# A transformer block on one core: operands of two pairs of features stay on chip between gate/up and down, weight loads move ahead of the next splits, and down's sums are stored two products later

## The chip, the cores and the metric

The kernel runs on one core of one Trainium2 chip. The core has five engines with a queue each: TensorE (PE, with its weight loads shown apart as PEld), VectorE (DVE), ScalarE (ACT), GpSimd (POOL) and SyncE (SP), which here only issues DMA transfers. The engines meet through semaphores. The metric is the device time of one execution in microseconds (us); the time before is the median of three executions.

## The reference

One layer of a decoder block over T = 512 tokens with 2048 channels, in float32:

```
h    = rms_norm(x, norm1_g)
proj = h @ w_in                     # split into heads of three token mixers
mix  = concat(dilated attention A, conformer convolution B, sliding attention C)
x    = x + mix @ w_out
h2   = rms_norm(x, norm2_g)
x    = x + (silu(h2 @ w_gate) * (h2 @ w_up)) @ w_down
```

The feed-forward width is 5632, that is 44 tiles of 128 features. The last line is the part in which the change lies. Its two stages are called gate/up and down here.

## The kernel before

**Precision.** A product of float32 operands is made from a high part (a copy to the type float32r) and a low part (the operand less its high part). For weights `split_up_to` makes them: ACT copies the weight to PSUM (`wn`, line 240) and to SBUF (`wh`, line 241), and DVE subtracts (`wl`, line 242). There are three buffers of each, and the split of a product is made two products ahead (`SPLIT_AHEAD`).

**Seven products in place of eight.** Gate/up and down multiply 2 x 2 blocks with a scheme of seven products, in the order `ORDER = (5, 1, 7, 6, 2, 4, 3)`. The 44 feature tiles are 22 *pairs* (tile p and tile p + 22); the 16 channel tiles are 8 pairs. A block of gate/up (`Wide`) is one pair of features of gate or of up: g0, u0, g1, u1, ... u21, so 44 blocks of seven products. A product is a run of matmuls of 128x512 with `wh` and one of 128x256 with `wl`, eight of each; the order of the two runs flips from product to product. A block of down (`Down`) is one pair of output tiles over a window of six to eight pairs of features. There are 24: three sweeps over the eight output pairs, and the list `DOWN` gives the windows, (0..5), (0..6), (1..7) and so on. The third sweep runs into pair 22, which is pair 0 again. Block d0 has 12 matmuls in a product, d1 has 14.

**Weights.** `group` lists, for each block, four raw weights to load (21, 22, 11, 12) and four sums over them, which are some of the seven factors: s = 21 + 22 four products before the block's first product, 21 += 11 three before, s -= 11 (in effect) at the first, s += 12 two after. They run on POOL, except for the group named `g0`, whose sums run on DVE. The raw weights lie in seven buffers by name; `pump` issues loads on SP for as long as the next entry's buffer is free. `next_unit` is called once per product: it runs the sums that are due, splits the weight of two products on, and then calls `pump`.

**Order within a product.** There is no scheduler: each engine runs its instructions in the order of the program (`manual_schedule`), so that the order of the calls sets the order in every queue. For each product the loop at the end of the kernel calls the sums, then `run(evacs)` (the previous product's results out of PSUM), then `next_unit`, then `multiply`, and then `run(extras)`. `later(n, ...)` puts a call n products further on in one of the two lists.

**Operands of down.** At the end of an up block, POOL, ACT and DVE make the seven operands of the pair from the four blocks of its result: `sums1` and `sums2` (POOL) and `piece1` to `piece4`. A piece makes one or two operands of high and low part (128x512 each) in a *stage* tile, of which there are two, and stores them to DRAM (`od[p]`, line 940 in the profile for the issue). `load_act` (issue at line 1116) brings operands back as tiles of 256 KB, `a{q}_{j}` for product q and pair j, in a pool of 71 *slots* of 2 KB per partition. A slot also holds normalised inputs, results and the y tiles, so the loads for d0 are called product by product in the last block of gate/up, as its inputs `ops` are dropped: six loads a product, 42 in all. Later blocks of down load the pairs that are new to their window. `load_y` reads the running sum of two output tiles (`x2d`) ahead of each block, `Down.done` adds to it, and `Down.store` writes it back, `later(0, ...)` on the list `extras`, that is in the same product.

**One queue.** All these transfers are issued by SP in the order of the program: raw weights (line 211), operands (1116), stage tiles (940), y (1069), and sums (1083).

Of the kernel before, what the change touches and what calls it, by code (L numbers as in the profile page):

```python
# [9 lines left out]
F32 = mybir.dt.float32  # L10
F32R = mybir.dt.float32r
# [4 lines left out]
P = 128  # L16
T = 512
# [26 lines left out]
        "bg3 ak2 cq4 ak0 av0 cq6 aq0 ak1 av1 aq1 av2 aq2 ak3 av3 aq3").split()  # L44
ROWS = "c0 c1 c2 c4 c5 c3 c7 c6 a0 a1 b2 b1 b0 b3 a2 a3".split()

N_SLOTS = 71

RAW_PLAIN = "22b sb 21 22a 11 sa 12".split()
RAW_BUFS = 7  # L50
RAW_EARLY = 5
# [11 lines left out]
TH = T // 2  # L63
NJ = KT // 2
NP = NF // 2


_A = [0, 0, 1, 2, 3, 4, 5, 6]
_B = [_A[n] + (6 if n == 0 else 7) for n in range(8)]
_C = [b + 8 for b in _B]  # L70
DOWN = [(n, *w) for ab in (zip(_A, _B), zip(_B, _C), zip(_C, [a + NP for a in _A])) for n, w in enumerate(ab)]

LAID = (5, 7, 6, 4, 3, 1, 2)
# [36 lines left out]
def kernel(ctx: ExitStack, tc: tile.TileContext, xT, wi, wo, wgu, wd, cst_in, outT):  # L110
    nc = tc.nc
    cp = ctx.enter_context(tc.tile_pool(name="consts", bufs=1))
    wp = ctx.enter_context(tc.tile_pool(name="weights", bufs=1))
    sp = ctx.enter_context(tc.tile_pool(name="slots", bufs=N_SLOTS))
    ctx.enter_context(tc.manual_schedule())
# [14 lines left out]
    def slot(name, dt=F32, cols=T):  # L130
        return sp.tile([P, cols], dt, name=name, tag="s")

    def bank(name, cols=T):
        return psum["banks"].tile([P, cols], F32, name=name, tag="b")
# [11 lines left out]
    def take(buf, key, n=1024):  # L146
        assert buf not in held
        held[buf] = key
        raws[key] = (wp.tile([P, 1024], F32, name=f"w{key}", tag=f"raw{buf}", bufs=1), n)
        return raws[key][0]  # L150

    def drop(key):
        for buf in [b for b, k in held.items() if k == key]:
            held.pop(buf)
        return raws.pop(key)
# [29 lines left out]
        works.extend((key[k], last, None) for k, last in (  # L185
            ("s", False), ("11", False), ("21", True), ("s", False), ("12", True), ("22", True), ("s", True)))

    for p in range(NP):
        for m in range(2):
            group(f"{'gu'[m]}{p}", m, 1024, {f"{i + 1}{k + 1}": [wgu[4 * (p + i * NP) + 2 * m + k]]  # L190
                                             for i in range(2) for k in range(2)})

    def down_block(n, half, first, end):

        parts = [(first, min(end, NP)), (0, end - NP)] if first < NP else [(first - NP, end - NP)]
        return [bass.AP(tensor=wd.tensor, offset=wd.offset + (n * P * NF + half * NP + a) * P,
                        ap=[[NF * P, P], [1, (b - a) * P]]) for a, b in parts if b > a]
# [6 lines left out]
    at = {"entry": 0, "split": 0, "use": 0}  # L204

    def pump(limit):
        while at["entry"] < len(entries) and len(raws) < limit and entries[at["entry"]][0] not in held:
            buf, key, parts = entries[at["entry"]]
            t, o = take(buf, key, sum(p.shape[-1] for p in parts)), 0
            for part in parts:  # L210
                nc.sync.dma_start(t[:, o:o + part.shape[-1]], part)
                o += part.shape[-1]
            at["entry"] += 1


    lows, late_lows = [], []

    def lows_now():
        while lows:
            fn, *args = lows.pop(0)  # L220
            fn(*args)  # L221
        if late_lows:
            pump(RAW_EARLY if at["use"] <= 20 else RAW_BUFS)

    def split_up_to(i):
        while at["split"] <= min(i, len(works) - 1):
            key, last, eng = works[at["split"]]
            t, n = drop(key) if last else raws[key]
            u = at["split"]
            hi = wp.tile([P, 1024], F32R, name=f"wh{u}", tag="hi", bufs=SPLIT_BUFS)  # L230
            lo = wp.tile([P, 1024], F32R, name=f"wl{u}", tag="lo", bufs=SPLIT_BUFS)
            if eng or "high" not in psum:
                eng = eng or nc.vector
                nc.scalar.copy(hi[:, :n], t[:, :n])  # L234
                lows.append((eng.tensor_sub, lo[:, :n], t[:, :n], hi[:, :n].bitcast(F32)))
                if not late_lows:
                    lows_now()
            else:
                near = psum["high"].tile([P, 1024], F32R, name=f"wn{u}", tag="h")
                nc.scalar.copy(near[:, :n], t[:, :n])  # L240
                nc.scalar.copy(hi[:, :n], t[:, :n])  # L241
                nc.vector.tensor_sub(lo[:, :n], t[:, :n], near[:, :n].bitcast(F32))
            splits[u] = (hi, lo)
            at["split"] += 1

    def sums_now():
        for fn in sums.pop(at["use"], ()):
            fn()

    def next_unit():  # L250
        sums_now()
        u = at["use"]
        at["use"] += 1
        lows_now()
        split_up_to(u + SPLIT_AHEAD)
        if not lows:
            pump(RAW_EARLY if u < 20 else RAW_BUFS)
        return splits.pop(u)

    def mm3(out, wh, wl, xh, xl, start, stop):  # L260
# [14 lines left out]
    for k in range(X_AHEAD):  # L275
        load_first(k)
        u = k if k < 2 else k // 2 + 1
# [100 lines left out]
    for k in range(KT):  # L378
# [9 lines left out]
        hi, lo = h_hl.pop(k)  # L388
# [14 lines left out]
    def project(name):  # L403
        b = bank(name)
        for half in range(2):
            wh, wl = next_unit()
            for kk in range(8):
                k = 8 * half + kk
                s = slice(kk * P, (kk + 1) * P)
                mm3(b, wh[:, s], wl[:, s], h_hi[k], h_lo[k], k == 0, k == KT - 1)  # L410
                if kk == 3:
                    lows_now()
                if kk % 2 == 1:
                    ticks.tick()
        return b
# [357 lines left out]
    for name in PROJ[HEAD4:]:  # L773
        kind, what, j = name[0], name[1], name[2:]
# [3 lines left out]
        b = project(name)  # L778
# [19 lines left out]
    b = box = boxes = shared = None  # L798
# [84 lines left out]
    for half in range(2):  # L883
        for i, n in enumerate(OUT_ORDER[half]):
            if half == 1 and i == 2:
                ticks.drain()
                b = None
                open_banks(banks=4, high=2)
            b = bank(f"o{half}_{n}")
            wh, wl = next_unit()  # L890
            for kk in range(8):
                k = 8 * half + kk
# [4 lines left out]
                s = slice(kk * P, (kk + 1) * P)  # L897
# [29 lines left out]
    def norm2b():  # L927
# [2 lines left out]
        nc.scalar.copy(R_12, b)  # L930
        nc.scalar.copy(r2b[:, T:], b[:, :TH])

    od = {p: tc.dram_tile([P, 7 * T], F32, name=f"od{p}") for p in range(NP)}
    evacs, extras = [], []
    flip = [1]
# [6 lines left out]
    def later(n, fn, *args, queue=evacs):  # L942
        while len(queue) <= n:
            queue.append([])
        queue[n].append((fn, *args))
# [35 lines left out]
    class Wide(Block):  # L981
# [54 lines left out]

        def piece(self, at, src):
            n = src.shape[-1] // TH
            both = wp.tile([P, 2 * T], F32R, name=f"{self.name}st{at}", tag="stage", bufs=2)
            near = psum["high"].tile([P, 1024], F32R, name=f"{self.name}n{at}", tag="h")[:, :n * TH]  # L1040
            hi, lo = (both[:, :n * T].rearrange("p (a b c) -> p a b c", a=n, b=2)[:, :, b] for b in range(2))
            src2, near2 = (t.rearrange("p (a b) -> p a b", a=n) for t in (src, near))
            nc.scalar.copy(near, src)
            nc.scalar.copy(hi, src2)
            nc.vector.tensor_sub(lo, src2, near2.bitcast(F32))
            later(0, nc.sync.dma_start, od[self.p][:, at * T:(at + n) * T], both[:, :n * T].bitcast(F32), queue=extras)

        def piece1(self):
            self.piece(0, self.ta)
# [21 lines left out]
    class Down(Block):  # L1071
# [9 lines left out]
        def store(self, n, t, cols):  # L1081
            def go():
                nc.sync.dma_start(self.out[n][:, cols], t[:, cols])
            if self.tail:
                go()
            else:
                later(0, go, queue=extras)

        def done(self, q):
            one, two = slice(0, TH), slice(TH, T)  # L1090
# [16 lines left out]
                self.add(q, t[:, cols])  # L1107
                self.store(n, t, cols)

    acts = {}  # L1110

    def load_act(q, pairs):
        for j in pairs:
            acts[q, j] = slot(f"a{q}_{j}", F32R)
            at = LAID.index(q)
            nc.sync.dma_start(acts[q, j].bitcast(F32), od[j % NP][:, at * T:(at + 1) * T])

    blk = gate = None
    for g in range(2 * NP + len(DOWN)):
        t = g - 2 * NP  # L1120
        if t < 0:
            p, m = divmod(g, 2)
            blk = Wide(p, m, gate if m else None)
            gate = blk if m == 0 else None
        else:
            n, first, end = DOWN[t]
            blk = Down(t)
        for i, q in enumerate(ORDER):
            sums_now()
            run(evacs)  # L1130
            w = next_unit()
            if t < 0:
                blk.multiply(q, w, [ops[q, j] for j in range(NJ)])
            else:
                blk.multiply(q, w, [acts[q, j] for j in range(first, end)])
            if g == 0 and i in (2, 3):
                (norm2a if i == 2 else norm2b)()

            if t == -1:
                for j in range(NJ):  # L1140
                    ops.pop((q, j))
                later(1, load_act, q, range(*DOWN[0][1:]), queue=extras)
            elif 0 <= t < len(DOWN) - 1:
                for j in range(first, DOWN[t + 1][1]):
                    acts.pop((q, j))
                later(1, load_act, q, range(end, DOWN[t + 1][2]), queue=extras)
            if t >= -1 and i == 3:
                load_y(t + 1)
            run(extras)
# [85 lines left out]
```

## Time and profile before

| | us |
|---|---|
| median of three executions | 1929.6 (1929.41 to 1929.71) |
| the profiled execution's own time | 1929.75 |
| its span, from the first instruction to the last | 1928.0 |
| PE busy | 1898.0 (98% of the span) |
| DVE, ACT, POOL busy | 1469.7, 1329.9, 985.9 |
| gate/up on PE | 623.0 to 1481.65 |
| down on PE | 1481.65 to about 1924.2 |
| waits of PE for operands from `od` | 5.3 in 13 waits, the longest 2.4 |
| loads of operands, `a<-od` | 196 of 256.0 KB, 5.4 us from issue to landing |

Reading it: a line of the profile names the program line, the engine, the operation, and output and inputs by the program's names; "x6" is a count of instructions that stand together, and what stands in brackets is the engine's idle time ahead of the instruction and what ended it. "L966" is the one line of all matmuls of gate/up and down; `out<-h` are those of gate/up and `out<-a` those of down. The clock is the share of its full rate that TensorE was granted. Weights are named by kind and block: `w('22', 'd1')` is the raw weight 22 of block d1. A chain in order of time gives start, duration, and what ran or was waited for.

### The profile page before, as it was taken

The page shows a single profiled execution, that of the slowest core. Times are in us where ns is not written, and L with a number is a line of the kernel's source. Part 1 is how long each engine was busy: PE and PEld are TensorE (multiplying, and loading weights), DVE is VectorE, ACT ScalarE, POOL GpSimd, SP SyncE. Part 2 cuts the span into 40 slices and gives each one's busy share as a digit, 9 for nine tenths or more (in the row PEclk, how much of TensorE's full clock was granted, in tenths as well). Part 3 has the DMA queues.
Part 4 walks back from the last instruction along what each step waited for, and adds up shares of the span by engine and source line. Part 5 has one row for each costly group of instructions (what it writes and reads, how often), then busy time and mean ns, then how long its engine had stood idle before and what let it go on. Part 6 is the DMA issues. An engine that isn't in the chain of part 4 may idle for free.

```text
span 1928.0 us, 29223 instructions
## 1 busy us (share of the span) xinstructions
PE 1898.0 (98%) x10332; PEld 1643.8 (85%) x10332; DVE 1469.7 (76%) x2512; ACT 1329.9 (69%) x1782; POOL 985.9 (51%) x636
## 2 busy tenths in 40 slices
PE   8999999999999999999999999999999999999999
PEld 7888788878877888888888888888888788888888
DVE  6799989997468777777777777777777577767776
ACT  6356555553356888788888888888887677667675
POOL 0111011000000788788887878788876666656564
PEclk9999999999999999999999999999999999999999
DMA  7222232223342344444444444454438988777685
GB/s 264 85 97 66 66 88 77 72 77 126 121 128 80 134 156 164 138 161 166 159 143 156 161 157 155 138 180 142 170 126 302 365 276 278 264 248 270 201 277 195
DMA packets 125651, 319.48 MB, mean 166 GB/s; under 512 B 14016, under 2 KB 29504, under 8 KB 125504
## 3 DMA queue, kind: packets, MB, share of 16 engines
q1 hardware_dynamic: 125360, 317.51, 48.1%
q8 instruction: 81, 1.33, 0.3%
q14 instruction: 66, 0.54, 0.1%
q10 hardware_dynamic: 144, 0.10, 0.0%
HBM read 259.09 MB, written 57.15 MB: 164 GB/s over the span
## 4 chain that ended last, share of the span: by engine, by line
PE 66%; DMA 1%; DVE 0%; ACT 0%; issue 0%; DVEq 0%; SPq 0%
PE out L966 66%; DMA a<-od 1%; DMA od<-u21st 0%; ACT wn L240 0%; DVE h L873 0%; ACT wh L241 0%; DVE ssum L90 0%; DVE xr L823 0%; PE n2b L301 0%; ACT h L867 0%; ACT h L833 0%; ACT sr L843 0%; PE r2s L307 0%; DVE tb L860 0%; DVE y L978 0%
## 5 line engine op out<-in xcount | busy, mean ns | idle before, releaser
L966 PE MATMUL out<-h,wh 128*128 128x512 f32 x2464 | 588.5, 391 | 3.6 <-DVE h L873 3.6
L966 PEld LDWEIGHTS out<-h,wh 128*128 128x128 f32 x2464 | 452.9, 188 | 91.6 <-DVE h L873 4.1
L966 PEld LDWEIGHTS out<-h,wl 128*128 128x128 f32 x2464 | 317.4, 192 | 12.0
L966 PE MATMUL out<-h,wl 128*128 128x256 f32 x2464 | 321.4, 284 | 0.0
L966 PE MATMUL out<-a,wh 128*128 128x512 f32 x1232 | 299.6, 393 | 3.5 <-DMA a<-od 3.1
L966 PEld LDWEIGHTS out<-a,wh 128*128 128x128 f32 x1232 | 226.9, 189 | 50.5 <-DMA a<-od 3.8
L234 ACT CAST wh<-w 128x1024 fp32r<-128x1024 f32 (+1 forms) x93 | 96.7, 1040 | 107.5 <-PE o L262 37.5
L966 PEld LDWEIGHTS out<-a,wl 128*128 128x128 f32 x1232 | 160.8, 193 | 10.5 <-DMA a<-od 4.0
L966 PE MATMUL out<-a,wl 128*128 128x256 f32 x1232 | 164.5, 285 | 2.2 <-DMA a<-od 2.2
L221 DVE TENSOR_TENSOR wl<-w,wh 128x1024 fp32r<-128x1024 f32 (+1 forms) x93 | 112.6, 1210 | 69.0 <-ACT wh L234 68.8
L978 DVE TENSOR_TENSOR y<-y,out 128x256 f32<-128x256 f32 x120 | 50.6, 421 | 65.6 <-PE out L966 62.6
L440 DVE SCALAR_TENSOR_TENSOR y<-bu,cst,y 128x511 f32<-128x511 f32 (+14 forms) x120 | 88.6, 739 | 0.5
L368 POOL TENSOR_TENSOR n2r<-n2v,nhalf 128x4 f32<-128x4 f32 x1 | 1.0, 1006 | 161.7 <-DVE n2v L367 161.7
L979 DVE TENSOR_TENSOR y<-y,out 128x256 f32<-128x256 f32 x120 | 50.5, 421 | 4.1
L262 PE MATMUL o<-ml_c,wh 128*128 128x512 f32 x128 | 51.0, 399 | 2.4 <-DVE ml_c L751 2.4
L261 PE MATMUL o<-mh_c,wh 128*128 128x512 f32 x128 | 51.7, 404 | 0.0
L261 PE MATMUL cq<-hh,wh 128*128 128x512 f32 x128 | 51.2, 400 | 0.0
L263 PE MATMUL o<-mh_c,wl 128*128 128x512 f32 x128 | 50.6, 395 | 0.0
L263 PE MATMUL cq<-hh,wl 128*128 128x512 f32 x128 | 50.0, 391 | 0.0
L262 PE MATMUL cq<-hl,wh 128*128 128x512 f32 x128 | 49.9, 390 | 0.0
L262 PEld LDWEIGHTS o<-ml_c,wh 128*128 128x128 f32 x128 | 24.5, 191 | 8.2 <-DVE ml_c L751 3.8
L261 PE MATMUL in<-hh,wh 128*128 128x512 f32 x64 | 25.8, 403 | 5.3 <-ACT wh L234 5.3
(3092 smaller groups left out, 4816.0 us busy)
## 6 DMA issues: line engine op xcount, KB each, us to landing
a<-od SPq DMA_DIRECT2D x196, 256.0 KB, 5.4
w<-in_wi SPq DMA_DIRECT2D x59, 512.0 KB, 3.6
w<-in_wo SPq DMA_DIRECT2D x32, 512.0 KB, 3.6
y<-x2d SPq DMA_DIRECT2D x48, 256.0 KB, 5.4
x2d<-y SPq DMA_DIRECT2D x64, 128.0 KB, 3.6
x<-in_xT SPq DMA_DIRECT2D x16, 256.0 KB, 7.2
xr<-in_xT SPq DMA_DIRECT2D x16, 256.0 KB, 3.8
x2d<-xr SPq DMA_DIRECT2D x16, 256.0 KB, 2.0
```

Of the source, the lines that this page charges most:

```text
L221: fn(*args)
L234: nc.scalar.copy(hi[:, :n], t[:, :n])
L261: nc.tensor.matmul(out, wh, xh, start=start, stop=False)
L262: nc.tensor.matmul(out, wh, xl, start=False, stop=False)
L263: nc.tensor.matmul(out, wl, xh, start=False, stop=stop)
L368: nc.gpsimd.tensor_tensor(r, v, nhalf[:, :NT], op=ALU.pow)
L440: nc.vector.scalar_tensor_tensor(yconv[j][:, i:], hconv[j][:, :T - i], c, yconv[j][:, i:], op0=ALU.mult, op1=ALU.add)
L966: nc.tensor.matmul(out, lhs[:, s], rhs, start=begin, stop=x is xs[-1] and low == flip[0], skip_group_check=True)
L978: sign(out, out if first is None else first, main)
L979: sign(out, out, rest)
```

## The change

1. **Order of the pairs.** Gate/up goes through the pairs in the order 1 to 5, 7 to 21, 0, 6 instead of 0 to 21. The groups of weights follow the same order. As the choice of the engine for the sums goes by the name `g0`, the sums of the first block (now g1) run on POOL and those of g0, now the second to last pair's, on DVE.
2. **Operands that stay.** `piece` puts each operand into a slot of its own, as the tile from which down multiplies, and the store to DRAM reads that slot. The stage tiles are gone, and there are 75 slots instead of 71. The copy of the high part and the subtraction are made per operand (256 wide) where they were made per piece (up to 512 wide), and a piece of two operands is stored in two transfers. The operands of the pairs 0 and 6 are kept in `acts`. Pair 0 is stored as well, as the third sweep reads it again; pair 6 is not stored. `load_act` leaves out what is there: d0 loads pairs 1 to 5 (35 loads), and pair 6 is not loaded for d1.
3. **Pump first.** In gate/up (from product 21 on) and in down `next_unit` calls `pump` ahead of `split_up_to`, not behind it. What the split of this product frees is thus filled in the next product's call.
4. **Stores of sums.** `Down.store` uses `later(2, ...)`, so that the store is issued two products later.

```diff
-N_SLOTS = 71
+N_SLOTS = 75
+GU_ORDER = [*range(1, 6), *range(7, NP), 0, 6]
+STAY = (0, 6)
...
-    for p in range(NP):
+    for p in GU_ORDER:
         for m in range(2):
             group(f"{'gu'[m]}{p}", m, 1024, ...
...
         lows_now()
+
+        if u > 20 and not late_lows:
+            pump(RAW_BUFS)
         split_up_to(u + SPLIT_AHEAD)
-        if not lows:
-            pump(RAW_EARLY if u < 20 else RAW_BUFS)
+        if u <= 20 and not late_lows:
+            pump(RAW_EARLY)
         return splits.pop(u)
...
         def piece(self, at, src):
             n = src.shape[-1] // TH
-            both = wp.tile([P, 2 * T], F32R, name=f"{self.name}st{at}", tag="stage", bufs=2)
             near = psum["high"].tile([P, 1024], F32R, name=f"{self.name}n{at}", tag="h")[:, :n * TH]
-            hi, lo = (both[:, :n * T].rearrange("p (a b c) -> p a b c", a=n, b=2)[:, :, b] for b in range(2))
-            src2, near2 = (t.rearrange("p (a b) -> p a b", a=n) for t in (src, near))
             nc.scalar.copy(near, src)
-            nc.scalar.copy(hi, src2)
-            nc.vector.tensor_sub(lo, src2, near2.bitcast(F32))
-            later(0, nc.sync.dma_start, od[self.p][:, at * T:(at + n) * T], both[:, :n * T].bitcast(F32), queue=extras)
+            for k in range(n):
+                q, s = LAID[at + k], slice(k * TH, (k + 1) * TH)
+                t = slot(f"a{q}_{self.p}", F32R)
+                nc.scalar.copy(t[:, :TH], src[:, s])
+                nc.vector.tensor_sub(t[:, TH:], src[:, s], near[:, s].bitcast(F32))
+                if self.p in STAY:
+                    acts[q, self.p] = t
+                if self.p != STAY[1]:
+                    later(0, nc.sync.dma_start, od[self.p][:, (at + k) * T:(at + k + 1) * T], t.bitcast(F32),
+                          queue=extras)
...
-                later(0, go, queue=extras)
+                later(2, go, queue=extras)
...
     def load_act(q, pairs):
         for j in pairs:
+            if (q, j) in acts or j == STAY[1]:
+                continue
             acts[q, j] = slot(f"a{q}_{j}", F32R)
...
-            p, m = divmod(g, 2)
+            p, m = GU_ORDER[g // 2], g % 2
```

More of the change, by code (lines that the diff above doesn't have):

```diff
@@ L931, in norm2b @@
         nc.scalar.copy(r2b[:, T:], b[:, :TH])
+    acts = {}
     od = {p: tc.dram_tile([P, 7 * T], F32, name=f"od{p}") for p in range(NP)}
@@ L1108, in done @@
                 self.store(n, t, cols)
-    acts = {}
     def load_act(q, pairs):
         for j in pairs:
+            if (q, j) in acts or j == STAY[1]:
+                continue
             acts[q, j] = slot(f"a{q}_{j}", F32R)
```

## The prediction

> **What bounds the kernel now.** The page's first and fourth parts come first: which engine is busy, and through what the chain that ended last runs.
>
> ```profile
> span 1928.0 us, 29223 instructions
> PE 1898.0 (98%) x10332; PEld 1643.8 (85%) x10332; DVE 1469.7 (76%) x2512; ACT 1329.9 (69%) x1782; POOL 985.9 (51%) x636
> ```
>
> TensorE has no room except in its waits. The chain in order of time tells where these are:
>
> ```profile
> 635.64 850.14 PE out L966 x4888
> ...
> 1496.62 6.72 DMA a<-od
> 1503.36 6.43 DMA od<-u21st
> ...
> 1512.16 412.01 PE out L966 x2366
> ```
>
> From 635.64 on, PE runs through gate/up and through down without a pause on the chain, except between 1485 and 1512, where transfers end last. This is where down starts: block d0 (from 1481.65) and the first product of d1. The change touches nothing else in which PE waits, so this stage was read closely. The windows (PE, its weight loads, DVE, ACT, POOL, then the granted clock, the DMA share and GB/s):
>
> ```profile
> 1400.00:1460.00 60.00, 60.00 (x348) 53.11 (x347) 44.91 (x63) 49.23 (x60) 47.81 (x33) 1.00 0.44 154
> 1481.00:1512.00 31.00, 25.40 (x102) 18.02 (x100) 13.68 (x23) 13.59 (x19) 14.27 (x12) 0.89 1.04 392
> 1500.36:1504.00 3.64, 0.98 (x2) 0.37 (x2) 0.00 (x0) 0.92 (x2) 2.95 (x2) 1.00 1.05 389
> 1504.00:1510.80 6.80, 6.75 (x21) 5.19 (x22) 2.01 (x3) 2.44 (x4) 6.72 (x7) 0.50 1.05 402
> 623.40:626.80 3.40, 3.40 (x18) 3.40 (x17) 3.33 (x10) 3.04 (x7) 0.00 (x0) 0.50 0.05 16
> ```
>
> In gate/up 60 us hold about 344.5 matmuls (348, 347 and 345 records in such windows), 174.2 ns each, so a product of 16 takes 2.787 us. The transition holds 84 matmuls of d0 and 14 of d1's first product: 98 x 0.1742 = 17.1 us needed, 30.5 taken (1481.65 to 1512.16), 13.4 us lost. Meanwhile the DMA is full (share 1.04, 392 GB/s, so a 256 KB load every 0.67 us). Last, the timelines of SP, POOL, ACT and PE:
>
> ```profile
> 1479.80 13.75 SPq L1116 DMA_DIRECT2D a<-od  x20
> 1493.94 0.33 SPq L211 DMA_DIRECT2D w('21', 'd1')_14819<-in_wd  x1
> 1494.53 0.33 SPq L211 DMA_DIRECT2D w('22', 'd1')_14821<-in_wd  x1
> ...
> 1496.00 5.22 SPq L1116 DMA_DIRECT2D a<-od  x7
> ```
>
> ```profile
> 1500.97 2.07 POOL L176 TENSOR_TENSOR w('s', 'd1')_14904<-w('21', 'd1')_14819,w('22', 'd1')_14821 128x896 f32<-128x896 f32 x1 [13.47 <-DMA w('22', 'd1')_14821<-in_wd]
> ```
>
> ```profile
> 1509.81 0.62 ACT L1044 CAST u21st<-u21tb 128x512 fp32r<-128x512 f32 x1 [0.41 <-DMA od<-u21st]
> 1510.34 0.90 ACT L240 CAST wn<-w('11', 'd1')_14823 128x896 fp32r<-128x896 f32 x1
> ```
>
> ```profile
> 1502.80 1.09 PE L966 MATMUL out<-a,wh 128*128 128x512 f32 x2 [2.44 <-DMA a<-od]
> 1512.16 1.88 PE L966 MATMUL out<-a,wh 128*128 128x512 f32 x7 [0.29 <-ACT wh L241]
> ```
>
> Two things end there nearly together: the operands of d0's last products, and behind them d1's weights. POOL idles 13.47 us for weight 22 of d1. Then, in its order, it does two weight sums (2.07, 2.09), three y adds (0.72 each) and the two sums of the last pair's tb; ACT makes the copies of tb (lines 1043, 1044) and only then wn and wh of d1's second product. From POOL's start to PE's second product of d1: 1512.16 - 1500.97 = 11.19 us.
>
> **The change part by part.**
>
> *Loads that go.* Pair 0 is not loaded for d0: 35 loads instead of 42. Alone that is 7 x 0.67 = 4.7 us less on the full queue. Pair 6 drops 7 loads for d1 and 7 stores of the last pair; these lie behind the decisive weights.
>
> *Order on SP.* With the pump ahead of the splits, a raw buffer that a product's split frees is filled one product later in program order. In the changed program's order on SP, weights 21, 22, 11 of d1 stand behind the loads of d0's last product (operands of product 3); before, they stood ahead of those (the rows at 1493.94 and 1496.00). So ahead of weight 22 there were 36 loads (six products of six), and now there are 35 (seven of five). The gain for this weight is not seven loads but one: 0.67 us. POOL then starts at 1500.97 - 0.67 = 1500.30.
>
> *d0 itself.* The last operand now lands ahead of both weights (458 KB, 1.17 us each): 1500.97 - 0.67 - 2.34 - 0.1 = 1497.9, against about 1506 (the last issue of the seven starts at about 1500.9, and the median landing is 5.4 us later). d0 ends near 1498.9 instead of about 1508. This gain goes into a wait: PE stands until d1's first weights are made. POOL 1500.30 to 1502.37, ACT wn and wh (0.84 apart, 0.93): d1's first product starts at about 1504.3, after 5.4 us of idle PE.
>
> *The second product of d1.* POOL's and ACT's order is unchanged. The chain of 11.19 us loses the wait for the stage tile (0.41, and 0.06 around it) since each operand has its own slot, and gains 0.09 because line 1044's copy is two of 256 (about 0.31 apart) instead of one of 512 (0.52 apart): 10.81 us. So PE goes on at 1500.30 + 10.81 = 1511.1, against 1512.16: **-1.05 us**.
>
> *Clock.* The granted clock was 0.50 in 1504.00:1510.80, behind a window with PE busy 0.98 of 3.64 us, and in 623.40:626.80, behind a sparse stretch too; these steps lie on a grid of 3.4 us. In the new order PE is idle 5.4 us before d1's first product and 2 to 3.6 us after it, so at 1511.1, where before the clock was full, it may be halved. A window of 3.4 us at half costs 1.7 us. The bounds are nothing and two windows (as long as 1504.00:1510.80), 3.4 us; I take one, **+1.7 us**. [...]
>
> *Splits of operands.* Per pair, three more small ACT copies and DVE subtractions, each about 0.1 us: hidden, since ACT is busy 49.2 and DVE 44.9 of 60 us. 22 pairs x 0.6 us on engines off the path: 0. Without that cover up to 13 us; nothing in 1400:1460 suggests it, as PE never waits.
>
> *Slots.* Two pairs hold 14 slots; four come from the stage tiles. The queue of loads keeps its pace as long as slots come free with the operands of gate/up, which happens product by product as before: 0.
>
> *Group order.* The group g0, whose four sums are on VectorE (1.22 us each for 128x1024), is now the second to last pair's. DVE there is idle 0.70 us per product: each sum puts it late by about 0.5 us, two in a row by 1.0, against splits made two products ahead: 0, bounds 0 and 4 x 1.22 = 4.9 us. At the start the sums of g1 go to POOL (2.41 us each), which is idle there; the DVE sums that go stood beside waits for ACT: 0, at best -0.1.
>
> *Stores two products later.* The x2d stores are read back eight blocks on; they leave SP's queue room for loads at first. Down's PE has no waits (the 412.01 us row): 0.
>
> *Pump order in the other blocks.* Same loads, at most a product later in the program; SP's issue is set by buffers coming free. Gate/up has a DMA share of 0.44; down has 0.65 to 0.85 with no PE wait: 0.
>
> Sum against the profiled execution (1929.75 us, 1928.0 of span and 1.75 around it): -1.05 + 1.7 gives 1930.4. The median of the three runs is 0.15 lower, 1929.6, so the forecast is **1930.2**.
>
> **The rivals.**
>
> *Faster, the loads count.* If weight 22 comes sooner by all seven loads (the chip's queue draws it forward, or SP issues it sooner than the order says), PE's second product starts 4.7 + 0.4 us earlier and no clock step is added: 1924.5. For it: the DMA is full throughout, so every byte taken out counts. Against it: a single queue, whose rows show issue in program order.
>
> *Faster, the transition closes.* If d0 and d1 run without waits, all 13.4 us go: 1916.2. Against it: POOL's chain of 11 us behind the weight cannot be hidden by d0's 14.6 us of matmuls unless the weight lands by 1485.
>
> *Slower, VectorE.* The four g0 sums reach PE. The place is blocks u21 and g0. It decides once DVE is late by more than the 2.8 us of one product. Its price is up to 4.9 us, and with the clock window 1935.1. Against it: 0.70 us of idle per product, 4.9 us over seven products.
>
> *Slower, the clock lasts.* Three or four windows at half behind 1511 cost 5.1 to 6.8 us: 1933.7 to 1935.4. For it: two idle stretches in a row, 5.4 and about 3 us. Against it: the longest halved stretch of the trace is 6.8 us.
>
> **How the numbers follow.** No change to the end 0.56 (1926.2 to 1932, with none to two windows and a weight landing up to 2 us sooner); seven loads count 0.15; transition closed 0.04; VectorE 0.12; clock lasts 0.13. A change of 0.2% (3.9 us) is about what a measurement of this kernel tells from none. Faster 0.19, within 0.56, slower 0.25. The range takes in 1924.5 and 1935.4 and leaves out the closed transition and the tails: 1924.0 to 1935.5.
>
> **What the changed profile would show.** SP: weight 21 of d1 behind all d0 loads. POOL's wait for weight 22 ends near 1500.3. PE idles near 1498.9 to 1504.3 for ACT or DVE (not for a) and starts d1's second product near 1511, the clock at 0.50 for one window after. No new wait for PE in blocks u21 and g0. The forecast is wrong if POOL starts before 1497, if PE waits in gate/up, or if the clock stays halved past 1518.

## The result and the profile after

The changed kernel takes 1937.8 us (median of six executions, 1935.25 to 1939.15) against 1929.8 for the kernel before (1929.41 to 1930.56): a ratio of 1.0037, with a 95% interval of 1.0026 to 1.0048. It is 8 us slower where 1930.2 was forecast, above the end of the range. The profiled execution took 1938.08 us, with a span of 1936.3.

The first lines of the page of the changed kernel: PE still has 98%, and its busy time is 3 us less than before (1898.0), so what was added is idle time.

```profile
span 1936.3 us, 29485 instructions
PE 1894.9 (98%) x10332; PEld 1644.2 (85%) x10332; DVE 1478.5 (76%) x2578; ACT 1334.7 (69%) x1848; POOL 985.2 (51%) x636
```

Its chain in order of time (start, duration, what ran), with the one piece of the chain before that is not shown yet ahead of it; the pieces at 635.64 and 1512.16 of before answer to those at 643.24 and 1519.03:

```profile
623.01 8.51 PE out L966 x41
```

```profile
629.26 9.85 PE out L974 x41
...
643.24 758.93 PE out L974 x4360
...
1408.82 82.20 PE out L974 x470
...
1519.03 413.57 PE out L974 x2366
```

Set beside the chain before, whose gate/up starts at 623.01 and 635.64, whose d0 starts at 1481.65 (now 1489.65) and whose last piece is 412.01 us at 1512.16, the 8.3 us of span come out as follows (the stretches sum to 8.4; behind the last matmul 0.1 us is lost less):

| stretch | before | after | difference |
|---|---|---|---|
| up to the piece of 41 matmuls of gate/up | 623.01 | 629.26 | +6.25 |
| from there to the piece that starts at 635.64 before | 12.63 | 13.98 | +1.35 |
| from there to d0 | 846.01 | 846.41 | +0.40 |
| d0 and the first product of d1 | 30.51 | 29.38 | -1.13 |
| the rest of down | 412.01 | 413.57 | +1.56 |

The transition, which the prediction was about, did what it said. The loss lies 870 us ahead of it, where gate/up starts. The timelines of POOL and DVE there, in the changed kernel, and behind them one row of DVE for the same subtraction in the kernel before, and the waits of PE, after and before:

```profile
588.05 2.50 POOL L180 TENSOR_TENSOR w('s', 'g1')_5633<-w('21', 'g1')_5391,w('22', 'g1')_5445 128x1024 f32<-128x1024 f32 x1 [116.50 <-DVE wl L225]
590.63 2.46 POOL L180 TENSOR_TENSOR w('21', 'g1')_5391<-w('21', 'g1')_5391,w('11', 'g1')_5494 128x1024 f32<-128x1024 f32 x1
614.94 2.45 POOL L180 TENSOR_TENSOR w('s', 'g1')_5633<-w('s', 'g1')_5633,w('11', 'g1')_5494 128x1024 f32<-128x1024 f32 x1 [21.85 <-DVE wl L246]
```

```profile
588.22 2.61 DVE L880 TENSOR_TENSOR h<-tb,h 128x256 fp32r<-128x256 f32 x1
590.76 2.61 DVE L880 TENSOR_TENSOR h<-h,h 128x256 fp32r<-128x256 f32 x1
593.29 0.41 DVE L880 TENSOR_TENSOR h<-tb,h 128x256 fp32r<-128x256 f32 x1
...
615.05 2.62 DVE L880 TENSOR_TENSOR h<-tb,h 128x256 fp32r<-128x256 f32 x1
617.59 0.41 DVE L880 TENSOR_TENSOR h<-h,h 128x256 fp32r<-128x256 f32 x1
```

```profile
588.43 0.42 DVE L873 TENSOR_TENSOR h<-tb,h 128x256 fp32r<-128x256 f32 x1
```

```profile
PE out L974 <- DVE h L880: 9.6, 2, 5.5
```

```profile
PE out L966 <- DVE h L873: 3.6, 1, 3.6
```

Line 880 (line 873 before) is the subtraction that makes the low parts of gate/up's inputs, both of its operands in SBUF (in tiles that the kernel does not take from its PSUM pools). It takes 0.41 us, and 2.61 or 2.62 us three times: each time it starts 0.1 to 0.2 us after a POOL sum and ends 0.3 us after it. Three times 2.2 us is 6.6 us, on the engine that makes the inputs for which PE waits: its waits for line 880 are 9.6 us in two waits, where before it was 3.6 in one. Row by row, DVE is 0.2 us ahead of before just before the first of the three (587.89 against 588.10), 4.2 us behind after the second (597.86 against 593.68) and 6.3 behind after the third (622.45 against 616.13). The fourth sum (635.89, 2.42 us) runs beside operations of DVE that read PSUM (lines 981 and 246), and these keep their 0.69 and 1.21 us. The late start also costs TensorE's clock two more full windows at 0.50, where both stood at 1.00 before (behind the length, the first number is PE's busy time; the granted clock is the third from the end):

```profile
626.80:630.20 3.40, 0.94 (x3) 0.84 (x4) 3.37 (x9) 2.08 (x5) 0.00 (x0) 0.50 0.21 77
630.20:633.60 3.40, 3.40 (x17) 3.40 (x16) 3.37 (x9) 3.40 (x8) 0.00 (x0) 0.50 0.00 0
```

The trace of before had shown the same thing elsewhere, in rows that the prediction did not look at. POOL's product in the convolution, and DVE beside it:

```profile
220.19 2.03 POOL L430 TENSOR_TENSOR bu<-bu,bg 128x512 f32<-128x512 f32 x1 [4.39 <-ACT bg L427]
```

```profile
219.88 1.22 DVE L221 TENSOR_TENSOR wl<-w,wh 128x1024 fp32r<-128x1024 f32 x1
221.01 1.74 DVE L440 SCALAR_TENSOR_TENSOR y<-bu,cst,y 128x488 f32<-128x488 f32 x1
```

The same operation of 487 elements has a mean of 720 ns; this one lasts until half a microsecond after POOL's end. POOL's operation itself is longer than the 1.30 us of a 128x512 product in gate/up (row at 1482.87); here DVE's `wl`, with both operands in SBUF, had begun 0.3 us ahead of it.

### The profile page after: what moved, and what is told of

Read it like the earlier page. It is cut to its first block, busy times and chain, and to the rows that moved or that the text cites. A ratio compares the mean times of both kernels' runs of the same rounds, so it can differ in the third digit from the quotient of the medians.

```text
span 1936.3 us, 29485 instructions
## 1 busy us (share of the span) xinstructions
PE 1894.9 (98%) x10332; PEld 1644.2 (85%) x10332; DVE 1478.5 (76%) x2578; ACT 1334.7 (69%) x1848; POOL 985.2 (51%) x636
## 4 chain that ended last, share of the span: by engine, by line
PE 70%; DMA 1%; DVE 1%; POOL 0%; ACT 0%; issue 0%; POOLq 0%; DVEq 0%; SPq 0%; ACTq 0%
PE out L974 65%; PE o L269 1%; PE o L270 1%; PE o L268 1%; DMA a<-od 1%; DMA w('22', 'd1')_15087<-in_wd 0%; DVE h L880 0%; DVE wl L246 0%; DVE xr L830 0%; POOL w('21', 'd1')_15085 L180 0%; ACT wn L244 0%; ACT wh L245 0%; DVE w('21', 'g0')_13992 L180 0%; POOL w('s', 'd1')_15138 L180 0%; DVE ssum L94 0%
```

## The experiments

**The first group's sums on VectorE again.** One name in the changed kernel:

```diff
-                eng = nc.vector if name == "g0" else nc.gpsimd
+                eng = nc.vector if name == "g1" else nc.gpsimd
```

> The changed kernel with one name altered: the sums of the first group (g1) run on VectorE, as the first group's did before, and those of g0 on GpSimd. Theory A (GpSimd's sums hold VectorE: in the changed kernel three subtractions of line 880 take 2.61 us instead of 0.42 beside them, 6.6 us, and the late start costs another step of the clock): the first product of gate/up starts at about 623 instead of 629, and the time falls by 6 to 8 us to 1930 to 1931.5; what is left above before is the step of the clock at the start of down, less the 0.7 us that the transition gains. Theory B (the start is late from the transfers or from the order of the pairs): no change, 1937.8. Theory C (the sums of g0 on VectorE, in the blocks u21 and g0, cost the time): the gain appears between 1400 and 1490 and the start stays at 629.

Measured: 1930.4 us (11 executions), a ratio to before of 1.0003 (0.9995 to 1.0012). Its chain:

```profile
622.51 8.50 PE out L974 x41
...
635.14 848.18 PE out L974 x4876
1511.15 414.74 PE out L974 x2366
```

Gate/up starts at 622.51 instead of 629.26, and no line 880 is stretched between 560 and 640 (means 416 and 417 ns). So the engine of these sums carries the whole slowdown. The rest of the change is worth nothing that this measurement can tell. The stretch from 635.14 to d0 at 1481.15 is 846.0 us, so that g0's sums on DVE cost the 0.4 us of the table and no more: the same stretch is 846.0 us in the traces of before and of five more kernels below in which g0 is the first group again or has its sums on POOL.

**The kernel before, with that alone.**

```diff
-                eng = nc.vector if name == "g0" else nc.gpsimd
+                eng = nc.gpsimd
```

> The kernel before with that side effect alone: the first group's four sums (g0) on GpSimd, nothing else changed. Theory A: slower by 6 to 8 us, 1936 to 1938, with two or three VectorE operations on SBUF operands of 2 to 2.6 us in place of 0.4 between 580 and 620. Theories B and C: 1929.8, no change.

Measured: 1936.9 us, a ratio of 1.0038 (1.0024 to 1.0051), the same as for the whole change. Its last piece of the chain:

```profile
1521.11 412.01 PE out L966 x2366
```

Gate/up starts at 630.76 there, PE waits 10.0 us for line 873, in two waits, and three rows of that line last 2.61 or 2.62 us, each beside a POOL sum. The side effect is enough for the slowdown, and without it the slowdown is gone.

**A POOL addition that nobody uses, and a memset in its place.** In the kernel before, behind each of the first two sums of g0 on VectorE, a POOL addition of one column of the sum fixes the time, and then comes either one addition of 128x768 or, in a second kernel, two memsets (`nc.gpsimd.memset(r2b, 0.0)`) of the same tile. The tile `r2b` is made and cleared earlier in the program for this, which is left out here:

```diff
                 eng.tensor_add(out[:, :n], raws[key[a]][0][:, :n], raws[key[b]][0][:, :n])
+                if name == "g0" and b in ("22", "11") and not last:
+                    nc.gpsimd.tensor_add(r2b[:, :1], r2b[:, :1], out[:, :1])
+                    nc.gpsimd.tensor_add(r2b, r2b, r2b)
...
```

> The kernel before, plus two GpSimd additions of 128x768 that nobody uses (in place on a constant tile, some 1.9 us each by the row of 1.85 us), started behind the first two sums of g0 on VectorE, at about 598.0 and 603.8. It tests the hold itself, with no weight depending on GpSimd. Theory A: the VectorE operations beside them (wl and h, both inputs in SBUF) stretch by up to 1.9 us each and the first product of gate/up starts 2 to 4 us later: 1931.5 to 1934. If it was the late sums as such that made the split wait and not a hold, no change, 1929.8.

> The same two places, but each addition is replaced by two GpSimd memsets of the same tile, which write SBUF and read nothing. If the hold comes with any GpSimd use of SBUF, VectorE's operations stretch here too and the time is 1931 to 1934; if it takes a GpSimd operation that reads SBUF, no stretch and 1929.8.

Measured: 1931.7 us with the addition, a ratio of 1.0009 (1.0000 to 1.0018), and 1930.8 with the memsets, 1.0002 (0.9993 to 1.0011). The times alone hardly part the two; the traces do. POOL and DVE with the addition:

```profile
599.42 2.37 POOL L179 TENSOR_TENSOR r2b<-r2b 128x768 f32<-128x768 f32 x1
...
606.23 1.14 POOL L178 TENSOR_TENSOR r2b<-r2b,w('21', 'g0')_5393 128x1 f32<-128x1 f32 x1 [4.44 <-DVE w('21', 'g0')_5393 L176]
607.45 1.53 POOL L179 TENSOR_TENSOR r2b<-r2b 128x768 f32<-128x768 f32 x1
```

```profile
599.24 1.23 DVE L224 TENSOR_TENSOR wl<-w,wh 128x1024 fp32r<-128x1024 f32 x1 [0.17 <-ACT wh L237]
600.38 1.69 DVE L878 TENSOR_TENSOR h<-ta,h 128x256 fp32r<-128x256 f32 x1
602.00 0.41 DVE L878 TENSOR_TENSOR h<-tb,h 128x256 fp32r<-128x256 f32 x1
...
606.10 1.23 DVE L224 TENSOR_TENSOR wl<-w,wh 128x1024 fp32r<-128x1024 f32 x1
607.24 0.42 DVE L878 TENSOR_TENSOR h<-ta,h 128x256 fp32r<-128x256 f32 x1
607.58 1.69 DVE L878 TENSOR_TENSOR h<-h,h 128x256 fp32r<-128x256 f32 x1
```

and with the memsets:

```profile
599.61 1.54 POOL L180 MEMSET r2b<- 128x768 f32 x2
```

```profile
600.59 0.42 DVE L879 TENSOR_TENSOR h<-ta,h 128x256 fp32r<-128x256 f32 x1
600.93 0.42 DVE L879 TENSOR_TENSOR h<-tb,h 128x256 fp32r<-128x256 f32 x1
```

Beside the addition one subtraction of DVE takes 1.69 us instead of 0.42, at each of the two places, though no weight depends on POOL; beside memsets of the same 1.5 us nothing is stretched. The first place shows the other direction too: DVE's `wl` began first (599.24) and kept its 1.23 us, and the POOL addition behind it took 2.37 us instead of 1.53. At the second place the addition of one column does the same: it starts after `wl` and takes 1.14 us, where at the first, ahead of `wl`, it took 0.19. In these rows the operation that started first kept its time (`wl` its 1.23 us, the second POOL addition its 1.53) and the one held was the one behind it (POOL's 2.37 and 1.14 us, DVE's 1.69).

The two subtractions were held for 1.27 us each, 2.5 us in all, within the expected 2 to 4. In the trace gate/up starts at 626.59, 3.6 us later than before, of which 1.0 stood already ahead of the first addition (DVE's first sum starts at 597.85, at 596.81 before). The median rose by only 1.5 us. The traced execution is the slowest of ten: five took 1930.7 to 1931.0 us and five 1932.4 to 1934.5. What parts them is not known, as only one was traced.

**The pump behind the splits again.** The kernel with g1's sums on VectorE, and `next_unit` as before:

```diff
-        if u > 20 and not late_lows:
-            pump(RAW_BUFS)
         split_up_to(u + SPLIT_AHEAD)
-        if u <= 20 and not late_lows:
-            pump(RAW_EARLY)
+        if not lows:
+            pump(RAW_EARLY if u < 20 else RAW_BUFS)
```

> The kernel with the first group's sums on VectorE (e1_first_on_dve, 1930.4 us), and the pump behind the splits again, as before. Weights 21, 22, 11 of d1 then stand on SP ahead of the five operand loads of d0's last product. Theory A (d1's weights behind the operands take the gain of the seven loads away): weight 22 lands 5 x 0.67 = 3.3 us sooner, POOL starts near 1496.5, d1's second product at about 1507.8 instead of 1511.2, and with shorter idle of PE the clock may keep its rate: 3.3 to 6 us off, 1924.5 to 1927. Theory B (the transition is set by something else, POOL's chain from its own inputs or the raw buffers coming free): within 1 us of 1930.4.

Measured: 1926.8 us, a ratio to before of 0.9983 (0.9974 to 0.9992). The kernel without this edit stood at 1.0003. POOL and the chain:

```profile
1497.46 2.07 POOL L180 TENSOR_TENSOR w('s', 'd1')_15140<-w('21', 'd1')_15059,w('22', 'd1')_15061 128x896 f32<-128x896 f32 x1 [9.93 <-DMA w('22', 'd1')_15061<-in_wd]
```

```profile
1508.29 412.01 PE out L971 x2366
```

From POOL's start to PE's second product it is 10.83 us, as in the prediction's sum (10.81), and the clock takes no step behind it (412.01 us). So the loads that the change takes out are worth about 3 us once d1's weights stand ahead of the last operands.

**The weights ahead of ten loads.** In addition the sixth product's operands are called for one product later:

```diff
-                later(1, load_act, q, range(*DOWN[0][1:]), queue=extras)
+                later(2 if i == 5 else 1, load_act, q, range(*DOWN[0][1:]), queue=extras)
```

> As e3_old_pump, and the operands of d0's sixth product are called for one product later too, so that d1's weights stand ahead of the loads of the last two products (ten loads). Theory A: weight 22 lands 6.7 us sooner than in e1_first_on_dve, POOL's chain of 10.8 us ends near 1504.5; the operands then land last, at about 1501.5, and d0 and the first product of d1 end near 1504.8: d1's second product at about 1504.8 and the time 1922 to 1925. Theory B: within 1 us of 1930.4.

Measured: 1925.0 us (1923.51 to 1926.22), 0.9972 of before (0.9960 to 0.9983). It is the fastest of all, though its interval overlaps that of the kernel ahead of it, so that a gain over that one is not shown. Now the operands of d0 are what PE waits for:

```profile
1495.17 3.35 PE L971 MATMUL out<-a,wl 128*128 128x256 f32 x5 [2.76 <-DMA a<-od]
```

From 1495 to 1501 the granted clock is 0.50; down goes on from 1498 without a wait for a weight.

**The pump first, alone, in the kernel before.**

```diff
+        if u > 20 and not late_lows:
+            pump(RAW_BUFS)
         split_up_to(u + SPLIT_AHEAD)
-        if not lows:
-            pump(RAW_EARLY if u < 20 else RAW_BUFS)
+        if u <= 20 and not late_lows:
+            pump(RAW_EARLY)
```

> The kernel before with the pump ahead of the splits alone: d1's weights 21, 22 and 11 stand behind all 42 operand loads of d0 instead of 36. Theory A: weight 22 lands 6 x 0.67 = 4 us later and d1's second product starts near 1516 instead of 1512.2, with an idle stretch of PE ahead of it that may halve the clock: slower by 4 to 7 us, 1934 to 1937. Theory B: no change, 1930.2.

Measured: 1935.5 us, 1.0031 (1.0019 to 1.0043).

```profile
1505.06 2.07 POOL L176 TENSOR_TENSOR w('s', 'd1')_14902<-w('21', 'd1')_14847,w('22', 'd1')_14849 128x896 f32<-128x896 f32 x1 [17.85 <-DMA w('22', 'd1')_14849<-in_wd]
```

POOL starts 4.1 us later than before (1500.97), as six loads of 0.67 us make it. The pump's move is a loss of 5 us by itself, and the change as a whole is not slower at this place only because the operands kept on chip pay for it.

**The stores in the same product again.** The kernel with g1's sums on VectorE, and `later(0, go, queue=extras)`.

> As e1_first_on_dve, with the stores of down's sums in the same product again instead of two later. The stores stand behind d1's weights on SP either way, and PE waits for nothing later in down: no change, 1930.4 within 1 us. If the delay serves the transition, slower by up to 2 us.

Measured: 1930.7 us, 1.0002 (0.9993 to 1.0011) beside 1930.4: the stores' delay is worth nothing that this measurement can tell.

## Why the prediction was wrong

- **The step that failed is "Group order".** It said of g1's sums that they go to POOL, "which is idle there", and of the DVE sums that go that they "stood beside waits for ACT: 0, at best -0.1". The durations were right (2.41 us predicted, 2.45 to 2.50 measured), and POOL was idle. The sums that leave DVE were indeed worth nothing: DVE lags by the same 4.18 us on both sides of the place where they stood. What was not asked is what a running POOL sum does to a DVE operation beside it. Measured: 6.25 us at the start of gate/up and 1.35 us after it for the clock, 7.6 of the 8.3 us. That step gave no bound for a loss at the start at all. Of the prediction's signs of being wrong, a wait of PE in gate/up came about, at its start and not in u21 and g0, where the prediction looked for it.
- **Why it could have been seen.** Before, the only POOL sums ran in stages whose DVE operations read PSUM, and DVE's rows beside them are not stretched (line 242 keeps 1.21 to 1.22 us for 128x1024). From these rows alone the cost would be put at zero. At the start of gate/up DVE's subtractions read SBUF twice, and the nearest rows for that are the convolution's (1.74 us against 0.72), which show the stretch. The runs show the same for this subtraction: 2.61 us instead of 0.41 beside sums, 1.69 instead of 0.42 beside the addition that nobody uses, 0.42 beside memsets, and POOL's 2.37 us instead of 1.53 where DVE was first. The trace of before held a row that spoke against this change, and the prediction did not weigh it.
- **Order on SP, d0 itself, the second product of d1: right.** In the kernel without the failed step POOL starts at 1500.37 (1500.30 predicted), PE idles 5.34 us ahead of d1's first product (5.4) and goes on with the second at 1511.15 (1511.1). That these clock times fit so closely is partly luck, since d0 began 0.5 us sooner in that execution. Counted from d0's start, the transition is 1.13 us shorter in the changed kernel (1.05 predicted), 0.51 in this one, and 1.25 in the one with the stores at once. That the gain is one load and not seven, since the pump's move puts d1's weights behind the operands, is shown from both sides by the two runs with the pump.
- **Clock: right in kind, and in size within its bounds.** +1.7 was taken, the author's estimate of one window at half; the last piece of the chain has 413.57 us against 412.01, +1.56, and 413.55 in the kernel with the stores at once. In the one with g1's sums on VectorE alone it is 414.74, +2.7, inside the bounds of 0 and 3.4. So the size differs between traces of the same order, and the one window taken is what two of these three show.
- **The sum without the failed step.** It forecast 0.6 us more than before; the kernel with g1's sums on VectorE stands 0.2 above before, with an interval of -1.0 to 2.3. One reading in it is off and changes nothing: 344.5 matmuls in 60 us is not the mean of the counts beside it (348, 347 and 345 give 346.7), which is 0.1 us in the 17.1.
- **VectorE's sums of g0** were given 0 with 4.9 as the other end: 0.40 us. **Stores**, **splits of operands**, **slots**: nothing, as said.
- **The rivals.** Both slower ones named a wrong mechanism: VectorE in u21 and g0 is worth 0.4 us, and a clock that lasts 1.6 to 2.7. The faster one by "all seven loads" did not come about in this change; the run with the weights ahead of ten loads has its size (5.1 us off, 4.7 + 0.4 worked out) by another route, since there PE goes on from d0 to d1 without waiting for a weight.

## What to carry to other kernels

When work moves from VectorE to GpSimd, look at what VectorE does beside it. Where both operands of VectorE's operations were in SBUF here, each one that began just after a GpSimd sum ended after that sum (2.6 us for an operation of 0.4), and that GpSimd was idle before said nothing on that. A choice of engine that hangs on a name ("g0") moves with an innocent reordering, so read what else a reordering selects. And a load taken out was worth its time here only to what stood behind it in the queue and was waited for (six loads more ahead of weight 22 put POOL's start 4.1 us later): count the loads ahead of the decisive transfer, before and after.

## What the runs showed of the hardware that was not expected

The clock stayed at half for four windows in a row in the kernel with g1's sums on VectorE, though PE was busy for most of each. Its windows (PE is the first number behind the length, the granted clock the third from the end):

```profile
1500.20:1503.60 3.40, 0.00 (x0) 0.00 (x0) 0.19 (x1) 1.13 (x2) 3.15 (x2) 1.00 0.46 171
1503.60:1507.02 3.42, 2.47 (x9) 2.33 (x10) 0.90 (x1) 0.65 (x1) 3.42 (x5) 0.50 0.23 75
1507.02:1510.43 3.41, 2.38 (x6) 1.32 (x4) 1.59 (x5) 2.25 (x5) 3.11 (x3) 0.50 0.01 2
1510.43:1513.85 3.42, 2.70 (x6) 2.16 (x7) 2.90 (x5) 3.42 (x5) 0.00 (x0) 0.50 0.00 0
1513.85:1517.26 3.41, 3.41 (x16) 3.28 (x15) 2.50 (x4) 3.41 (x6) 2.11 (x1) 0.50 0.86 276
1517.26:1520.67 3.41, 3.41 (x18) 2.85 (x17) 1.95 (x5) 1.83 (x3) 1.36 (x1) 1.00 1.02 366
```

Here windows of 70 to 79% busy (2.38 to 2.70 us) were followed by another at half, and the first full one (3.41 us) by one at 1.00. The rate was lost behind a window in which PE did nothing (0.00 us). In the kernel before, a window with 0.98 of 3.40 us busy was followed by half the rate, and one with 3.35 of 3.40 us (1504.00 to 1507.40) by one more at half. How busy a window has to be, if that is what decides, was not tried. Whether such steps are why executions of one kernel differ (1935.25 to 1939.15 for the changed kernel) is not shown: of its six executions the one with the lowest mean clock, 0.989, took 1938.09 us, and the slowest, 1939.15, had 0.993 like the one of 1937.52.
